# Ordinary products for the left half's last pairs, a skewed right half, and activation sums and two weight sums on GpSimd, in a two-layer hybrid decoder

## The chip, the cores and the metric

The kernel runs on one core of a Trainium2 chip. The metric is the device time of one execution in microseconds. PE is TensorE, DVE VectorE, ACT ScalarE, POOL GpSimd and SP SyncE, whose queue issues nearly all DMA transfers.

## The reference

Two layers over 256 tokens of width 2048, in float32. Every layer computes

```
h  = RMSNorm(x)
P  = h @ W_in            # [q | k | v | gate_B | gate_C | conv_in]
A  = differential attention(q, k, v)
Cv = gate_B * causal_conv3(gate_C * conv_in)
x  = x + concat([A, Cv]) @ W_out
x  = x + (relu(RMSNorm(x) @ W_up) ** 2) @ W_down     # W_up 2048x8192, W_down 8192x2048
```

The change touches only the last line, the MLP.

## The kernel before

**Precision.** Each float32 operand of a matmul is split into a high part (a rounding copy on ACT, the "h" or "hi" tiles) and a low part (a subtraction on DVE, the "l" or "lo" tiles). A product is three matmuls, `TERMS` = high x high, high x low, low x high. So every weight that comes from HBM costs one ACT copy and one DVE subtraction of the same size (L281 and L282 for the projections and w_down's right half, L692 and L693 for w_up, L707 and L708 for the left half's forms).

**The walk over pairs.** `mlp` goes over 8192 hidden columns in NP = 32 pairs of 128. For a pair i, `up_column` computes two columns a and b of 128 (32 matmuls each, in two halves of 8 k-tiles, weights from `Weights.take`), into a PSUM bank "av" of which there is one; `evict` copies it by ACT and adds its two parts by DVE (L788). `square` then makes relu, the factor of the norm (L796) and the square, writes the result to DRAM by POOL's queue (`hid`, L799), makes four sums S1 to S4 of 128x128 on DVE (L800 to L803) and splits all eight matrices into f (L805 on ACT, L806 on DVE).

**The left half's products.** Columns 0 to 1023 of the output are made by a scheme with seven products for a 2x2 block product instead of eight. The weights' side of pair j needs a 512-column block split for b11, b21, b22 (`plain`), sums t of the weight blocks (`sums`: L724 makes t[:, 0:2], L727 and L728 the other two), and their splits t13 and t24 (L707, L708). The 21 matmuls of pair j = i - LAG, with LAG = 2, stand behind the columns of pair i: four products behind column a, three behind column b. The seven results stay in seven PSUM banks over the whole walk. Two pairs of products remain after the last columns. Then `onto` and additions combine them into x.

**The right half.** Columns 1024 to 2047 are ordinary products: for each pair, `back` reads hid from DRAM, ACT and DVE split it (L885, L886), and 24 matmuls (L892) go into two accumulators of two banks. Weights come as `draw` tiles of 256 rows by 1024 columns (1 MB).

**What sets the order.** PE's order is that of the program text. The orders of DVE, ACT, POOL and SP are set by a scheduler when the program is built, except for instructions marked `late`, which stay in program order. Each engine then goes through its own queue strictly in order. `Weights` keeps a list of jobs (`column`, `plain`, `sums`, `more`, `rows`) and makes AHEAD = 3 of them ahead of their use. `wpool` has three buffers each for hi and lo. A tile of a pool that was opened where another pool had closed can be written only when the old pool's users are done: `upool` (w_up's raw tiles), `spool` (split forms and t), `fpool` (h and f) and `dpool` (draw) are opened in this order at the start of the MLP, over the projections' pools.

Of the kernel before, what the change touches and what calls it, by code (L numbers as in the profile page):

```python
# [9 lines left out]
F32 = mybir.dt.float32  # L10
# [24 lines left out]
LAG = 2  # L35

# [64 lines left out]
def trunk(ctx: ExitStack, tc: tile.TileContext, x, w_in, w_out, conv_w, q_norm_g, k_norm_g,  # L101
# [564 lines left out]
    def mlp(l, mnorm, last):  # L666
# [3 lines left out]
        with ExitStack() as scope:  # L670
            upool = scope.enter_context(tc.tile_pool(name="upool", bufs=3))
            spool = scope.enter_context(tc.tile_pool(name="spool", bufs=1))
# [5 lines left out]
            weights = Weights(upool)  # L678
            raws, forms = {}, {}
# [24 lines left out]
            def parts(src, tag, bufs):  # L704
                hi = spool.tile(list(src.shape), F32R, tag=f"{tag}h", name=f"{tag}h", bufs=bufs)
                lo = spool.tile(list(src.shape), F32R, tag=f"{tag}l", name=f"{tag}l", bufs=bufs)
                nc.scalar.activation(hi, src, AF.Copy)  # L707
                nc.vector.tensor_sub(lo, src, hi.bitcast(F32))  # L708
                return hi, lo

            def quarters(i):


                def plain():
                    raw = forms["raw"] = load_rows(i, 0).rearrange("p k (n c) -> p k n c", n=2)
                    h1, l1 = parts(raw[:, 0, 0], "b1", 2)
                    h2, l2 = parts(raw[:, 1], "b2", 1)
                    return (h1, l1), (h2[:, 0], l2[:, 0]), (h2[:, 1], l2[:, 1])

                def sums():  # L720
                    raw = forms["raw"]
                    t = forms["t"] = spool.tile([P, 4, CH], F32, tag="t", name="t")

                    nc.vector.tensor_sub(t[:, 0:2], raw[:, :, 1], raw[:, 0])  # L724
                    h, lw = parts(t[:, 0:2], "t13", 1)

                    nc.vector.tensor_add(t[:, 2], t[:, 1], raw[:, 0, 0])  # L727
                    nc.vector.tensor_sub(t[:, 3], raw[:, 1, 0], t[:, 2])  # L728
                    return (h[:, 0], lw[:, 0]), (h[:, 1], lw[:, 1])

                def more():
                    h, lw = parts(forms["t"][:, 2:4], "t24", 1)
                    return (h[:, 0], lw[:, 0]), (h[:, 1], lw[:, 1])

                return plain, sums, more

            def rows(i, k, box):
                def make():
                    if k == 0:
                        box.append(load_rows(i, 2 * CH))  # L740
# [3 lines left out]
            for i in range(NP + LAG):  # L744
                plain, sums, more = quarters(i - LAG)
                if i < NP:
                    column(i, 0, 0)
                    column(i, 0, 1)
                if i >= LAG:
                    weights.jobs += [plain, sums]  # L750
                if i < NP:
                    column(i, 1, 0)
                    column(i, 1, 1)
                if i >= LAG:
                    weights.jobs.append(more)
            for i in range(NP):
                box = []
# [4 lines left out]
            hid = [dram.tile([P, 2 * S], F32, name=f"hid{l}{i}") for i in range(NP)]  # L762

            def up_column(name, warm):


                acc = (bank(name) if warm else ps.tile([P, CH], F32, tag="av", name=name, bufs=1))
                acc = acc.rearrange("p (h s) -> p h s", h=2)
                for kh in range(2):
                    hi, lo = weights.take()  # L770
                    for part, wt in ((0, hi), (1, lo)):
                        for k in range(8):
                            a = mT[kh * 2 + k // KG]
                            while not a.ready:
                                work.tick()
                            nc.tensor.matmul(  # L776
                                acc[:, 0] if part else acc, wt[:, k],
                                a.ap[:, 0, k % KG] if part else a.ap[:, :, k % KG],
                                start=(part == 0 and kh == 0 and k == 0),
                                stop=(part == 1 and kh == 1 and k == 7), skip_group_check=True)  # L780
                            if k % 4 == 3:
                                work.tick()
                return acc

            def evict(acc, dst):
                ev = nat.tile([P, 2, S], F32, tag="wide", name="ev")
                nc.scalar.activation(ev, acc, AF.Copy)
                nc.vector.tensor_add(dst, ev[:, 0], ev[:, 1])  # L788

            def square(i, h):  # L790
# [8 lines left out]
                nc.gpsimd.dma_start(hid[i], u)  # L799
                nc.vector.tensor_add(h[:, S1], h[:, A21], h[:, A22])  # L800
# [4 lines left out]
                nc.scalar.activation(f[:, 0], h, AF.Copy)  # L805
                nc.vector.tensor_sub(f[:, 1], h, f[:, 0].bitcast(F32))  # L806
                return f

            prods = []

            def product(n, i, a, b):

                f = fs[i]
                for m, (pa, pw) in enumerate(TERMS):
                    nc.tensor.matmul(prods[n], f[:, pa, a], b[pw], start=(i == 0 and m == 0),  # L815
                                     stop=(i == NP - 1 and m == 2))

            fs = {}
            h = None
            for i in range(NP + LAG):  # L820
                j = i - LAG
                if i < NP:
                    h = fpool.tile([P, 8, P], F32, tag="h", name="h", bufs=1)
                    evict(up_column(f"up{l}{i}a", i < LAG),
                          h[:, 0:2].rearrange("p a c -> p (a c)"))
                if j == 0:
                    wides = [mm.tile([P, 2, CH], F32, tag="mm2", name=f"pr{l}{n}")
                             for n in range(2)]
                    prods += [wides[0][:, 0], wides[0][:, 1], wides[1][:, 0], wides[1][:, 1]]
                    prods += [bank(f"pr{l}{n}") for n in (5, 6, 7)]  # L830
                if j >= 0:
                    b11, b21, b22 = weights.take()
                    t1, t3 = weights.take()
                    product(0, j, A11, b11)
                    product(1, j, A12, b21)
                    product(2, j, S4, b22)
                    product(4, j, S1, t1)
                    work.tick()
                if i < NP:
                    evict(up_column(f"up{l}{i}b", i < LAG),  # L840
                          h[:, 2:4].rearrange("p a c -> p (a c)"))
                    fs[i] = square(i, h)
                if j >= 0:
                    t2, t4 = weights.take()
                    product(6, j, S3, t3)
                    product(5, j, S2, t2)
                    product(3, j, A22, t4)
                    work.tick()


            p1, p2, p3, p4, p5, p6, p7 = prods
# [5 lines left out]
            e1 = wide("e1")  # L857
            nc.scalar.activation(e1, p1, AF.Copy, scale=mnorm.scale)
            onto(xs[0][:, 0], p2, xs[0][:, 0])
            onto(xs[1][:, 0], p3, xs[1][:, 0])  # L860
            onto(xs[0][:, 1], p4, xs[0][:, 1])
            u2, u3, u4 = wide("u2"), wide("u3"), wide("u4")
            onto(u2, p6, e1)
            onto(u3, p7, u2)
            onto(u4, p5, u2)
            onto(xs[1][:, 1], p5, xs[1][:, 1])
            for dst, v in ((xs[0][:, 0], e1), (xs[1][:, 0], u4), (xs[0][:, 1], u3),
                           (xs[1][:, 1], u3)):
                nc.vector.tensor_add(dst, dst, v)
            if last:  # L870
                for n in range(2):
                    for t in range(NT):
                        nc.sync.dma_start(
                            out[0, t * P:(t + 1) * P, n * CH:(n + 1) * CH], xs[n][:, t])
# [5 lines left out]
            acc = [mm.tile([P, NT, CH], F32, tag="mm2", name=f"dn{l}{n}") for n in range(2)]  # L880
            for i in range(NP):
                back = nat.tile([P, 2, S], F32, tag="wide", name="back")
                nc.sync.dma_start(back.rearrange("p k s -> p (k s)"), hid[i])
                f = fpool.tile([P, 2, 2, S], F32R, tag="f", name="fr")
                nc.scalar.activation(f[:, 0], back, AF.Copy)  # L885
                nc.vector.tensor_sub(f[:, 1], back, f[:, 0].bitcast(F32))  # L886
                for k in range(2):
# [63 lines left out]
```

## Time and profile before

| what | us |
|---|---|
| median of 3 runs | 2214.55 (2214.05 to 2215.54) |
| the profiled execution | 2216.24 |
| its span | 2214.4 |
| mean granted TensorE clock | 0.989 of full speed |

The span is the time from the first to the last instruction; 1.84 us lie around it. The page gives each engine's busy time; PE's instructions are pipelined, so that a matmul shows 0.39 us but follows its predecessor by 0.227 to 0.229 us. The marks of layer 0 in the trace: the o projection ends at 398.97, the last up column of the walk at 905.41, the first matmul of the right half starts at 932.52. In layer 1 the last up column ends at 2008.04, the first matmul of the right half starts at 2031.12, and the last accumulation ends at 2211.24. The lines "idle before <-releaser" in the timeline tell how long an engine stood still before an instruction and which engine's instruction ended that.

### The profile page before, as it was taken

Reading aid. Unit: us, or ns where it says so; the run is one execution under the profiler, and the core shown is the slowest. Engines: PE = TensorE matmul, PEld = TensorE weight load, DVE = VectorE, ACT = ScalarE, POOL = GpSimd, SP = SyncE. Lnnn points to the kernel's source line nnn. Section 1 sums busy time; section 2 is a strip of 40 time slices with the busy share of each in tenths; the row PEclk is TensorE's granted clock in tenths of the full one; section 3 lists DMA queues with packets and bytes.
Section 4 is the critical chain, followed back from the end, with each engine's and each line's share of the span. In section 5 each row is a group of like instructions: output and inputs, shape, how many; then the busy total and the mean of one; then the engine's idle time right before and its main releaser. Section 6 shows DMA issues by size and latency. Waiting matters only on the chain.

```text
span 2214.4 us, 29244 instructions
## 1 busy us (share of the span) xinstructions
PE 2167.4 (98%) x11054; PEld 1836.7 (83%) x11054; DVE 1631.7 (74%) x2303; ACT 1296.1 (59%) x1758; POOL 130.7 (6%) x186
## 2 busy tenths in 40 slices
PE   8999999999999999799999999999999999998999
PEld 6888888788888888688878888887888888886887
DVE  6677655789898989665556776557989898987555
ACT  6455445566666666454454654446666666664443
POOL 2021200000000000000010111000000000000000
PEclk9999999999999999899999999999999999998999
DMA  7656666566766666477565566656666666665774
GB/s 259 180 153 194 202 185 180 190 218 206 221 211 217 215 212 202 166 234 241 185 191 180 159 197 197 188 164 205 217 212 216 215 213 219 211 198 161 244 244 164
DMA packets 280717, 446.64 MB, mean 202 GB/s; under 512 B 10915, under 2 KB 191733, under 8 KB 280576
## 3 DMA queue, kind: packets, MB, share of 16 engines
q1 hardware_dynamic: 273872, 423.66, 61.7%
q0 software_dynamic: 6656, 21.10, 2.5%
q8 instruction: 86, 1.41, 0.3%
q14 instruction: 55, 0.45, 0.1%
q10 hardware_dynamic: 48, 0.02, 0.0%
HBM read 425.84 MB, written 18.90 MB: 201 GB/s over the span
## 4 chain that ended last, share of the span: by engine, by line
PE 96%; DMA 1%; DVE 1%; ACT 0%; issue 0%; POOL 0%; SPq 0%; DVEq 0%
PE dn L892 16%; PE pr L815 14%; PE o L337 8%; PE gc L359 4%; PE ci L359 4%; PE q L337 4%; PE gb L359 4%; PE v L337 4%; PE k L337 4%; DMA draw<-in_w_down_dram 1%; PE sc L499 1%; PE av L535 1%; PE tpn L401 0%; DVE wlo L282 0%; PE ptp L525 0%; PE up00b L776 0%
## 5 line engine op out<-in xcount | busy, mean ns | idle before, releaser
L282 DVE TENSOR_TENSOR wlo<-raw,whi 128x1024 fp32r<-128x1024 f32 (+1 forms) x258 | 317.1, 1231 | 244.3 <-ACT whi L281 243.1
L281 ACT ACTIVATE whi<-raw 128x1024 fp32r<-128x1024 f32 (+1 forms) x258 | 271.3, 1053 | 311.8 <-PE o L337 73.6
L692 ACT ACTIVATE uhi<-uraw 128x1024 fp32r<-128x1024 f32 x256 | 270.6, 1057 | 304.4 <-PE o L337 10.0
L693 DVE TENSOR_TENSOR ulo<-uraw,uhi 128x1024 fp32r<-128x1024 f32 x256 | 312.6, 1221 | 110.9 <-ACT uhi L692 106.7
L892 PE MATMUL dn<-whi,fr 128*128 128x512 f32 x1024 | 319.9, 393 | 9.5 <-ACT fr L885 7.0
L282 DVE TENSOR_TENSOR wlo<-draw,whi 128x1024 fp32r<-128x1024 f32 x128 | 156.9, 1225 | 150.7 <-ACT whi L281 150.6
L281 ACT ACTIVATE whi<-draw 128x1024 fp32r<-128x1024 f32 x128 | 135.7, 1061 | 174.4 <-PE dn L892 168.4
L892 PEld LDWEIGHTS dn<-whi,fr 128*128 128x128 f32 x1024 | 194.3, 190 | 51.4 <-ACT fr L885 7.9
L892 PE MATMUL dn<-wlo,fr 128*128 128x512 f32 x512 | 200.8, 392 | 0.0
L337 PE MATMUL o<-whi,cat 128*128 128x512 f32 x512 | 159.6, 390 | 0.0
L892 PEld LDWEIGHTS dn<-wlo,fr 128*128 128x128 f32 x512 | 97.2, 190 | 20.1
L337 PEld LDWEIGHTS o<-whi,cat 128*128 128x128 f32 x512 | 96.1, 188 | 19.8
L815 PE MATMUL pr<-t13h,f 128*128 128x512 f32 x256 | 100.5, 395 | 0.0
L337 PE MATMUL o<-wlo,cat 128*128 128x512 f32 x256 | 99.6, 389 | 0.0
L799 POOL DMA_DIRECT2D hid<-h x64 | 34.8, 544 | 985.4 <-ACT h L798 985.4
L815 PE MATMUL pr<-b2h,f 128*128 128x512 f32 x256 | 91.4, 398 | 0.0
L337 PE MATMUL q<-whi,nT 128*128 128x512 f32 x256 | 87.0, 409 | 3.3 <-ACT nT L247 2.1
L815 PE MATMUL pr<-t24h,f 128*128 128x512 f32 x256 | 89.6, 391 | 0.0
L337 PE MATMUL k<-whi,nT 128*128 128x512 f32 x256 | 85.3, 399 | 0.0
L337 PE MATMUL v<-whi,nT 128*128 128x512 f32 x256 | 83.4, 396 | 0.0
L708 DVE TENSOR_TENSOR t24l<-t,t24h 128x1024 fp32r<-128x1024 f32 x64 | 78.4, 1225 | 3.5 <-ACT t24h L707 0.4
L708 DVE TENSOR_TENSOR t13l<-t,t13h 128x1024 fp32r<-128x1024 f32 x64 | 78.4, 1224 | 3.5 <-ACT t13h L707 1.5
(953 smaller groups left out, 4667.8 us busy)
## 6 DMA issues: line engine op xcount, KB each, us to landing
uraw<-in_w_up_dram SPq DMA_DIRECT2D x128, 1024.0 KB, 5.8
draw<-in_w_down_dram SPq DMA_DIRECT2D x128, 1024.0 KB, 5.1
raw<-in_w_in_dram SPq DMA_DIRECT2D x192, 512.0 KB, 3.9
raw<-in_w_out_dram SPq DMA_DIRECT2D x64, 512.0 KB, 3.6
hid<-h POOLq DMA_DIRECT2D x64, 256.0 KB, 3.5
back<-hid SPq DMA_DIRECT2D x64, 256.0 KB, 2.7
rev<-by_dist_d POOLq DMA_DIRECT2D x4, 1024.0 KB, 10.6
out_dram<-x SPq DMA_DIRECT2D x8, 256.0 KB, 2.3
```

Of the source, the lines that this page charges most:

```text
L281: nc.scalar.activation(hi[:, k], raw[:, k], AF.Copy)
L282: nc.vector.tensor_sub(lo[:, k], raw[:, k], hi[:, k].bitcast(F32))
L337: nc.tensor.matmul(acc[:, t], a.ap[:, pa, k % KG, t * P:(t + 1) * P], (hi, lo)[pw][:, j], start=(k == 0 and n == 0), stop=(k == nk - 1 and ...
L359: nc.tensor.matmul(acc[:, f, 0] if part else acc[:, f], wt[:, k % 4, fs], a.ap[:, 0, k % KG] if part else a.ap[:, :, k % KG], start=(part ...
L499: nc.tensor.matmul(sc[:, :W], qT[m * DK:(m + 1) * DK, a, i, t * P:(t + 1) * P], kT[m * DK:(m + 1) * DK, b, i, :W], start=(n == 0), stop=(n ...
L535: nc.tensor.matmul(av[:, i * P:(i + 1) * P], pT[:, a, k * P:(k + 1) * P], v[:, b, k, i * P:(i + 1) * P], start=(k == 0 and n == 0), stop=( ...
L692: nc.scalar.activation(hi, src, AF.Copy)
L693: nc.vector.tensor_sub(lo, src, hi.bitcast(F32))
L708: nc.vector.tensor_sub(lo, src, hi.bitcast(F32))
L799: nc.gpsimd.dma_start(hid[i], u)
L815: nc.tensor.matmul(prods[n], f[:, pa, a], b[pw], start=(i == 0 and m == 0), stop=(i == NP - 1 and m == 2))
L892: nc.tensor.matmul(acc[n][:, t], f[:, pa, k, t * P:(t + 1) * P], b[pw][:, n], start=(i == 0 and k == 0 and m == 0), stop=(i == NP - 1 and ...
```

## The change

The change has six parts, all of them in `mlp`.

1. The last LAG = 2 pairs of the left half are ordinary products (eight products, 24 matmuls, instead of seven and 21), after the last up column; pairs 0 to 29 keep the seven products.
2. The right half goes in 16 blocks of 512 rows. Its two 512-column halves n = 0 and n = 1 are skewed: (0,0), (1,0), (0,1), (2,0), (1,1) and so on. Weights come as 512 KB chunks (`weights.straight`), hid as 512 KB blocks. The half n = 0 ends one block before n = 1.
3. POOL makes S1 to S4 (four 128x128 operations for a pair) and t[:, 0:2] (now two operations of 128x512), and the four additions of the products to x.
4. The columns of pair 0 are computed with the k-half as the outer loop, in one tile with two accumulators, and the splits and sums of pair 0 are `late`.
5. The draw load of pair i + 1 is issued in `sums` of pair i.
6. `fpool` and `dpool` are opened first, then a stack `first` with `spool` and `upool`, which is closed ahead of the right half; `rpool` and `gpool` (the right half's chunks and blocks) then take its place.

```diff
+            fpool = scope.enter_context(tc.tile_pool(name="fpool", bufs=2))
+            dpool = scope.enter_context(tc.tile_pool(name="dpool", bufs=2))
+            first = scope.enter_context(ExitStack())
+            spool = first.enter_context(tc.tile_pool(name="spool", bufs=1))
+            upool = first.enter_context(tc.tile_pool(name="upool", bufs=3))
...
-                    nc.vector.tensor_sub(t[:, 0:2], raw[:, :, 1], raw[:, 0])
+                    for m in range(2):
+                        keep(nc.gpsimd.tensor_tensor(t[:, m], raw[:, m, 1], raw[:, 0, m],
+                                                     op=ALU.subtract))
                     h, lw = parts(t[:, 0:2], "t13", 1)
...
+                    if i + 1 < NP - LAG:
+                        loads[i + 1]()
...
             for i in range(NP):
+                pair = quarters(i - LAG)
+                if i == 0:
+                    for kh in range(2):
+                        for c in range(2):
+                            column(0, c, kh)
+                    continue
...
+            order = [(b - n, n) for b in range(NB2 + 1) for n in range(2) if 0 <= b - n < NB2]
+            for b, n in order:
+                weights.straight(w_down[l], b * KG * P, KG, (2 + n) * CH)
...
-                nc.vector.tensor_add(h[:, S1], h[:, A21], h[:, A22])
-                nc.vector.tensor_sub(h[:, S2], h[:, S1], h[:, A11])
-                nc.vector.tensor_sub(h[:, S3], h[:, A11], h[:, A21])
-                nc.vector.tensor_sub(h[:, S4], h[:, A12], h[:, S2])
+                n = 4
+                if i < NP - LAG:
+                    n = 8
+                    for dst, a, b, op in ((S1, A21, A22, ALU.add), (S2, S1, A11, ALU.subtract),
+                                          (S3, A11, A21, ALU.subtract),
+                                          (S4, A12, S2, ALU.subtract)):
+                        nc.gpsimd.tensor_tensor(h[:, dst], h[:, a], h[:, b], op=op)
...
+            first.close()
+            rpool = scope.enter_context(tc.tile_pool(name="rpool", bufs=RAW))
+            gpool = scope.enter_context(tc.tile_pool(name="gpool", bufs=3))
+            weights.pool = rpool
...
+            for dst, v in ((x11, e1), (x12, e4), (x21, e3), (x22, e3)):
+                nc.gpsimd.tensor_tensor(dst, dst, v, op=ALU.add)
...
+            for j in range(NP - LAG, NP):
+                for k in range(2):
+                    b = weights.take()
+                    for n, t, p in ((0, 0, 2), (0, 1, 4), (1, 0, 3), (1, 1, 8)):
+                        for m, (pa, pw) in enumerate(TERMS):
+                            nc.tensor.matmul(
+                                prods[p], fs[j][:, pa, 2 * k + t], b[pw][:, n],
+                                start=(p == 8 and j == NP - LAG and k == 0 and m == 0),
+                                stop=(j == NP - 1 and k == 1 and m == 2))
```

In the queues of the changed program the two parts that moved to POOL stand as follows. At the start of the walk: hid(0), the sums of pair 0, hid(1), the sums of pair 1, t of pairs 0, 1 and 2, hid(2), the sums of pair 2. In the walk, for each pair: hid, two sums, two operations of t for a later pair, two sums. On ACT, the square of pair 1 stands behind the eviction of the first column of pair 2, and the split t13 of pair 0 behind that square and f(1). The first three loads of w_up in a layer wait for the end of the o projection, and the first two draw loads stand ahead of them on SP.

More of the change, by code (lines that the diff above doesn't have):

```diff
@@ L733, in more @@
                     return (h[:, 0], lw[:, 0]), (h[:, 1], lw[:, 1])
+                loads[i] = load
                 return plain, sums, more
@@ L759, in mlp, with column_bank, up_part @@
                 rows(i, 1, box)
[L762 to L783, printed above, removed]
+            order = [(b - n, n) for b in range(NB2 + 1) for n in range(2) if 0 <= b - n < NB2]
+            for b, n in order:
+                weights.straight(w_down[l], b * KG * P, KG, (2 + n) * CH)
+            hid = [dram.tile([P, KG * S], F32, name=f"hid{l}{b}") for b in range(NB2)]
+            def column_bank():
+                acc = ps.tile([P, CH], F32, tag="av", name="upc", bufs=1)
+                return acc.rearrange("p (h s) -> p h s", h=2)
+            def up_part(acc, kh):
+                hi, lo = weights.take()
+                for part, wt in ((0, hi), (1, lo)):
+                    for k in range(8):
+                        a = mT[kh * 2 + k // KG]
+                        while not a.ready:
+                            work.tick()
+                        nc.tensor.matmul(
+                            acc[:, 0] if part else acc, wt[:, k],
+                            a.ap[:, 0, k % KG] if part else a.ap[:, :, k % KG],
+                            start=(part == 0 and kh == 0 and k == 0),
+                            stop=(part == 1 and kh == 1 and k == 7), skip_group_check=True)
+                        if k % 4 == 3:
+                            work.tick()
             def evict(acc, dst):
@@ L814, in product @@
+            prods = {}
+            def product(n, j, a, b, stop=False):
                 for m, (pa, pw) in enumerate(TERMS):
-                    nc.tensor.matmul(prods[n], f[:, pa, a], b[pw], start=(i == 0 and m == 0),
-                                     stop=(i == NP - 1 and m == 2))
+                    nc.tensor.matmul(prods[n], fs[j][:, pa, a], b[pw], start=(j == 0 and m == 0),
+                                     stop=(stop and m == 2))
             fs = {}
-            h = None
-            for i in range(NP + LAG):
+            for i in range(NP):
@@ L821, in mlp @@
                 j = i - LAG
[L822 to L851, printed above, removed]
+                end = i == NP - 1
+                h = fpool.tile([P, 8, P], F32, tag="h", name="h", bufs=1)
+                if i == 0:
+                    two = mm.tile([P, 2, CH], F32, tag="mm2", name="up0")
+                    two = [two[:, c].rearrange("p (h s) -> p h s", h=2) for c in range(2)]
+                    for kh in range(2):
+                        for c in range(2):
+                            up_part(two[c], kh)
+                            if kh:
+                                evict(two[c], h[:, 2 * c:2 * c + 2])
+                    fs[0] = square(0, h)
+                    continue
@@ new lines, in mlp @@
+                for c in range(2):
+                    if i < LAG:
+                        acc = bank("upw").rearrange("p (h s) -> p h s", h=2)
+                    else:
+                        acc = column_bank()
+                    up_part(acc, 0)
+                    up_part(acc, 1)
+                    evict(acc, h[:, 2 * c:2 * c + 2])
+                    if c == 1:
+                        fs[i] = square(i, h)
+                    if j == 0 and c == 0:
+                        for pair in ((1, 6), (2, 3)):
+                            w2 = mm.tile([P, 2, CH], F32, tag="mm2", name=f"pr{l}{pair[0]}")
+                            prods[pair[0]], prods[pair[1]] = w2[:, 0], w2[:, 1]
+                        for n in (4, 5, 7):
+                            prods[n] = bank(f"pr{l}{n}")
+                    if j >= 0 and c == 0:
+                        b11, b21, b22 = weights.take()
+                        t1, t3 = weights.take()
+                        product(1, j, A11, b11, end)
+                        product(2, j, A12, b21)
+                        product(3, j, S4, b22)
+                        product(5, j, S1, t1, end)
+                        work.tick()
+                    elif j >= 0:
+                        t2, t4 = weights.take()
+                        product(7, j, S3, t3, end)
+                        product(6, j, S2, t2, end)
+                        product(4, j, A22, t4)
+                        work.tick()
@@ L853, in onto @@
+            blocks = {0: block(0)}
             def onto(dst, p, base):
@@ L870, in mlp, with store @@
+            for dst, p in ((x11, 2), (x21, 4), (x12, 3), (x22, 8)):
+                onto(dst, prods[p], dst)
+            def store(n):
+                for t in range(NT):
+                    nc.sync.dma_start(
+                        out[0, t * P:(t + 1) * P, n * CH:(n + 1) * CH], xs[n][:, t])
             if last:
[L871 to L874, printed above, removed]
+                store(0)
+                store(1)
@@ L877, in mlp @@
                 work.start(norm.chunk(1, 2), 24)
[L880 to L887, printed above, removed]
-                    b = weights.take()
-                    for n in range(2):
+            accs = {}
+            for b, n in order:
+                if n == 0:
+                    if b + 1 < NB2:
+                        blocks[b + 1] = block(b + 1)
+                if b == 0:
+                    accs[n] = mm.tile([P, NT, CH], F32, tag="mm2", name=f"dn{l}{n}")
+                f, acc = blocks[b], accs[n]
+                for kp in range(KG // 2):
+                    hi, lo = weights.take()
+                    for k in (2 * kp, 2 * kp + 1):
                         for t in range(NT):
```

113 lines of the change are left out of this document (56 added, 57 removed).

## Prediction

> **What bounds the kernel now.** I read the page's shares and chain first, then the waits of PE, then the timeline of one steady pair and of each seam.
>
> ```profile
> PE 2167.4 (98%) x11054; PEld 1836.7 (83%) x11054; DVE 1631.7 (74%) x2303; ACT 1296.1 (59%) x1758; POOL 130.7 (6%) x186
> ...
> PE 96%; DMA 1%; DVE 1%; ACT 0%; issue 0%; POOL 0%; SPq 0%; DVEq 0%
> ```
>
> PE is the path. Only two things shorten it: fewer matmuls, or fewer gaps. The waits of PE show the gaps:
>
> ```profile
> PE pr L815 <- ACT f L805: 9.8, 2, 5.0
> PE dn L892 <- ACT fr L885: 7.0, 2, 5.6
> PE up00a L776 <- DVE nT L248: 4.7, 2, 3.7
> PE up10a L776 <- DVE nT L248: 4.6, 2, 3.6
> ...
> PE tpn L401 <- DVE nT L248: 3.0, 1, 3.0
> PE dn L892 <- DVE fr L886: 2.5, 1, 2.5
> ```
>
> (total, times, longest). They lie at three seams, none in the walk over the pairs. PE's timeline at layer 0's seam before the right half:
>
> ```profile
> 904.81 0.76 PE L776 MATMUL up031b<-nT,ulo 128*128 128x256 f32 x5
> ...
> 918.64 0.79 PE L815 MATMUL pr<-b1h,f 128*128 128x512 f32 x1 [4.80 <-ACT f L805]
> ...
> 932.52 0.80 PE L892 MATMUL dn<-whi,fr 128*128 128x512 f32 x1 [5.55 <-ACT fr L885]
> ```
>
> After each long idle some 14 matmuls come 0.427 us apart instead of 0.227: 2.8 us more, so a gap costs more than its wait.
>
> Last, DVE in a steady pair (two of its operations, and its only idle):
>
> ```profile
> 703.03 0.28 DVE L800 TENSOR_TENSOR h<-h 128x128 f32<-128x128 f32 x1
> ...
> 703.44 1.22 DVE L724 TENSOR_TENSOR t<-draw 128x1024 f32<-128x1024 f32 x1
> ...
> 714.61 1.23 DVE L693 TENSOR_TENSOR ulo<-uraw,uhi 128x1024 fp32r<-128x1024 f32 x1 [1.62 <-ACT uhi L692]
> ```
>
> A pair takes 15.93 us on PE (two up columns of 5.56, 21 products of 0.229). DVE is idle for 1.62 of it, so busy 14.31.
>
> **The seam before the right half: -29 us.** The last column ends at 905.41. 51 products x 0.227 = 11.6 should end at 917.0. The right half, counted back from 939.10 by its 16 matmuls at 0.228, begins in effect at 935.45: 18.4 lost. Layer 1: 2008.04 + 11.6 = 2019.65 against 2035.54, 15.9 lost. After: pair 29's nine products, then 48 ordinary ones, so the right half starts 57 x 0.227 = 12.9 us after the column. That is 6 products more than before, 1.36 us. Pair 31's f is needed at 33 x 0.227 = 7.5; its chain (eviction 0.6, addition 0.42, relu 0.54, ratio 0.42, square 0.54, f 0.54, 0.6) sums to 3.7, some 6 with hand-overs and other work in the queues. Blocks and straight chunks can load only after the products' pool is free, at 2.05: 512 KB takes 3.9 (the raw row), the two splits 1.05 + 1.22, so 8.2 to 9 against 12.9. Both fit. Saved: (18.4 + 15.9) - 2 x 1.36 = 31.6; up to 6 off for slips, I take 29 (25 to 31). The cover is those 48 products; where it fails, the rival below.
>
> **Layer boundary and end: -5.7.** Between the layers 6.25 is lost (idles of 1.1 and 3.0 and the slow start after them). With the first 512 columns finished a block (24 matmuls, 5.5 us) earlier, most of the norm's chain and one PSUM buffer come earlier: -5 (-3 to -6). At the end two of four accumulations of about 0.7 go behind PE's last block: -0.7.
>
> **The start of the MLP: +5.** The stacks of pools change places: the buffers of the up weights now lie where the projections' tiles were, so SP issues the first three up loads only when the o phase is done. In the profile that moment is 399.21, where the draw load L699 with the same wait was issued. In exchange draws come early, at about 393. A 1 MB up load lands 5.8 after issue: 405.0 to 406, uhi 1.06, so PE starts at about 406.5 instead of 398.97. That idle is 7.5; with 2.8 of slow matmuls, less 1.1 of transposes that it covers, 9.2 is lost. Before, the stretch 398.97 to 412.49 held 6.64 of work, so 7.0 (layer 1: 6.6) was lost. Net +2.4 per layer (0 to +5). The order with k-half outermost hides the last nT, which caused the old idle.
>
> **The first product of t13: +19.** This is a new wait. POOL's queue has hid(1), the four sums of pair 1, and only then t(0); ACT's has square(1) behind the eviction of pair 2's first column. From the end of that column: the eviction ends at 0.75, square at 1.3, POOL starts at 1.6, issues hid for 0.54 (L799 row), four sums at 0.3 to 0.4 each (bounds 0.20 from the 128x4 rows of POOL, 0.61 from its 128x256 row), two halves of t at 1.29 (POOL's 128x512 row, L645), then t13h 1.05. That is 7.4 if nobody interferes. DVE's split of f(1) falls between the halves of t: about 1.1 more, 8.5. PE has nine products, 2.06, as cover: 6.4 idle, about 1 for t13l, 2.8 of slow matmuls, less what overlaps: 9.5 per layer (8 to 11). Before, t came from DVE early and there was no wait. Queued behind t13h on ACT are t24h and the next uhi; five later microseconds of column cover those.
>
> **The steady pairs: +4.** DVE loses four sums (0.81 by their starts) and L724 (1.13): 12.37 stays. POOL gets 4 x 0.3 to 0.4 and 2 x 1.29: 3.8 to 4.2 of work. Alone both fit in 15.93. Together they may not:
>
> ```profile
> 211.26 1.29 POOL L645 TENSOR_TENSOR gc01w<-gc01w,rowb 128x512 f32<-128x512 f32 x1 [1.47 <-PE ci L359]
> ```
>
> ```profile
> 211.31 2.33 DVE L282 TENSOR_TENSOR wlo<-raw,whi 128x1024 fp32r<-128x1024 f32 x1 [0.19 <-ACT whi L281]
> ```
>
> DVE's split took 2.33 instead of 1.23 because it began 0.05 after POOL's product: it stood still for 1.1 of POOL's 1.29. Elsewhere POOL's L582 took 4.42 against three splits back to back. So the two run in turn, each hand-over saving about 0.14. All DVE operations of a pair are of that kind (two SBUF tensors). Then a pair costs DVE 12.37 + 2 x 1.15 + 4 x 0.2 = 15.5, against 15.93. It fits by 0.4 us, and PE has three weight tiles of reserve. I take the row's hand-over (nearest, the same pair of engines) and 0.07 us in each of 60 pairs for places where the order catches them badly: +4 in all (0 to +37).
>
> The Trainium skill says the same of the pair: in "SBUF — State Buffer", section "Who interferes with whom", a DVE instruction with two SBUF inputs contends with a GpSimd one that reads SBUF, and the first to start holds it for the whole instruction. The trace agrees in kind (2.33 against 1.23); by the page's whole-instruction lock no hand-over is saved, which is the first rival. "GPSIMD Engine Reference", section "Engine selection", also advises VectorE for elementwise work, GpSimd being about twice as slow; here 1.29 against 0.68 for 128x512.
>
> **The sum.** -29 - 5.7 + 5 + 19 + 4 = -6.7 on the profiled span of 2214.4: 2207.7. That execution took 2216.24, 1.84 around its span and 1.7 above the median of 2214.55; I take the change from the median: 2207.9, say 2208. The likeliest case's own range, with its terms not all at the same end, is 2200 to 2218.
>
> **Rival 1: DVE and POOL become the bound (slower).** If the hand-over saves nothing, a pair costs 12.37 + 2.58 + 1.6 (sums at 0.40) = 16.55, 0.62 above 15.93; from 15.93 on every pair is late. 60 pairs give +37, in place of +4: 2241. For it: only 0.4 us of room, and POOL's results feed DVE's own next steps. Against: the 0.14 seen at each hand-over. Chance 0.22.
>
> **Rival 2: the new waits at the start are small (faster).** If t(0) reached ACT before the column ended, or up loads were on chip when the o phase ends, the 24 go: 2184 for both, 2194 for half. The queue order speaks against it: hid(1) stands ahead of t(0). Chance 0.13.
>
> **Rival 3: the seam stays (slower).** If the first block or straight chunk is split later than 12.9 us after the column, PE idles there as it did. Each microsecond counts once, with 2.8 more from some 4 us on. With the old idle of 5.6 + 2.8 in both layers, +17 on the forecast: 2225. For it: these loads cannot be issued before 2.05, and ACT and DVE are then busy with pair 31 and the products' evictions. Against: 4 us of slack. Chance 0.15.
>
> **How the numbers follow.** A measurement of this kernel tells about 0.2% (4.4 us) from no change. The forecast has 0.50: 2200 to 2218 reaches over both bounds, and I give 0.30 of it to faster, 0.14 to the same, 0.06 to slower. With rival 2's 0.13 faster has 0.43; with 0.02 of the weak form of rival 3 the same has 0.16; the rest, 0.22 + 0.13 + 0.06, is 0.41 slower. Cases of both signs hold most of the chance. The range reaches from half of rival 2, 2194, to a little past rival 1, 2246.
>
> **What would show it.** Right: PE's waits of pr on f and of dn on fr fall under 2 us per layer; the first up column waits 7 to 8 us for uhi; one wait of 5 to 7 us per layer for t13h; steady pairs of 15.9 to 16.0 us; DVE operations in them now and then 0.3 to 1.2 longer. Wrong: a pair period of 16.5 (rival 1), no wait for t13h (rival 2), dn still waiting for its blocks (rival 3), or a wait at pairs 3 and 4 that I have not costed.

## Result and the profile after

The changed kernel is slower: 2233.88 us (2233.57 to 2234.50, 4 runs) beside 2215.05 for the kernel before on the same chip, ratio 1.0082 (95% interval 1.0070 to 1.0095). The forecast was 2208, inside a range of 2194 to 2246: the sign was wrong, the range held the time. Of the rivals, the first (DVE and GpSimd become the bound) came true in its mechanism; its time was 2241.

The page's busy times and PE's waits (total, times, longest) of the changed kernel:

```profile
PE 2175.4 (97%) x11066; PEld 1831.5 (82%) x11066; DVE 1700.5 (76%) x1929; ACT 1260.7 (56%) x1718; POOL 451.4 (20%) x554
```

```profile
PE up L799 <- ACT uhi L694: 18.0, 2, 9.2
PE pr L839 <- ACT t13h L714: 14.7, 2, 7.4
PE upc L799 <- ACT ev L809: 7.8, 39, 0.2
```

DVE executes 374 instructions fewer and is busy 69 us longer; an operation that stands still counts as busy. The waits on f and fr at the seam before the right half are gone. Three others are there: the first up column for its weights, the first t13, and, new, some 40 short waits for the eviction of a pair's first column.

Stage by stage, from the starts of PE's matmuls in both traces (from one mark to the next, layer 0 and layer 1; the right half's start before the change is counted back over its slow matmuls, as in the prediction):

| stage | before | after | difference | forecast |
|---|---|---|---|---|
| end of o phase to the third column's end (first products) | 36.07, 35.66 | 40.82, 42.00 | +11.1 | +5 |
| from there to the end of the last column: first t13 | | | +20.9 | +19 |
| the same: the later pairs | | | +20.5 | +4 |
| last column to right half | 30.04, 27.50 | 13.95, 13.97 | -29.6 | -29 |
| right half of layer 0 to end of next o phase | 566.56 | 560.57 | -6.0 | -5 |
| right half of layer 1 to the end of the span | 178.86 | 178.97 | +0.1 | -0.7 |

With +0.5 from before the MLP this makes +17.5; the spans of the two profiled executions differ by 17.4 (2214.4 and 2231.8), the medians by 18.8. The stretch of the pairs is 470.37 before and 491.04 after in both layers. It splits by the distance from one pair's first product to the next: the first is 26.72 and 25.99 instead of 15.93, the next seven to nine are 15.93, and from about the tenth on all are 16.43.

One such pair on DVE and GpSimd, and the PE wait in it:

```profile
709.14 1.23 DVE L715 TENSOR_TENSOR t24l<-t,t24h 128x1024 fp32r<-128x1024 f32 x1 [0.18 <-ACT t24h L714]
710.61 6.17 DVE L695 TENSOR_TENSOR ulo<-uraw,uhi 128x1024 fp32r<-128x1024 f32 x2 [0.25 <-ACT uhi L694]
716.70 0.68 DVE L715 TENSOR_TENSOR b1l<-draw,b1h 128x512 fp32r<-128x512 f32 x1
```

```profile
710.50 0.89 POOL L828 TENSOR_TENSOR h<-h 128x128 f32<-128x128 f32 x2
711.34 2.53 POOL L734 TENSOR_TENSOR t<-draw 128x512 f32<-128x512 f32 x2
713.84 1.86 POOL L828 TENSOR_TENSOR h<-h 128x128 f32<-128x128 f32 x2
```

```profile
712.05 2.12 PE L799 MATMUL upc<-nT,uhi 128*128 128x512 f32 x8 [0.20 <-ACT ev L809]
```

Two splits that take 2.35 us back to back take 6.17: DVE stands still for 3.8 us, while GpSimd does five of its six operations, and the two lie one behind the other. Nearly all of it falls on the first split alone:

```profile
710.61 4.77 DVE L695 TENSOR_TENSOR ulo<-uraw,uhi 128x1024 fp32r<-128x1024 f32 x1 [0.25 <-ACT uhi L694]
```

It starts 0.11 after GpSimd's first sum and gets on only when the fifth operation ends, at 714.29. DVE's other operations in the pair follow each other with next to no gap; its only idle is 0.18 + 0.25. DVE is full, its later work comes late, so ACT's copies do, and PE's next column waits for the eviction that clears its only bank. DVE repeats every 16.4 from the third pair on, PE at first every 15.93: the split t24l starts 13.3 us before PE uses its result, half a microsecond less with each pair, and 9.55 from about the tenth on. This lead is the reserve that covers the first pairs.

### The profile page after: what moved, and what is told of

Same layout as the page of the kernel before. It is cut to its first block, busy times and chain, and to the rows that moved or that the text cites. A ratio compares the mean times of both kernels' runs of the same rounds, so it can differ in the third digit from the quotient of the medians.

```text
span 2231.8 us, 29487 instructions
## 1 busy us (share of the span) xinstructions
PE 2175.4 (97%) x11066; PEld 1831.5 (82%) x11066; DVE 1700.5 (76%) x1929; ACT 1260.7 (56%) x1718; POOL 451.4 (20%) x554
## 5 line engine op out<-in xcount | busy, mean ns | idle before, releaser
L283 DVE TENSOR_TENSOR wlo<-raw,whi 128x1024 fp32r<-128x1024 f32 (+1 forms) x386 | 473.3, 1227 | 385.8 <-ACT whi L282 384.5
L695 DVE TENSOR_TENSOR ulo<-uraw,uhi 128x1024 fp32r<-128x1024 f32 x256 | 517.5, 2038 | 45.0 <-ACT uhi L694 44.2
L799 PE MATMUL upc<-nT,uhi 128*128 128x512 f32 x1920 | 485.9, 395 | 8.0 <-ACT ev L809 7.8
L799 PEld LDWEIGHTS upc<-nT,uhi 128*128 128x128 f32 x1920 | 351.4, 189 | 92.6 <-ACT ev L809 25.6
L960 PE MATMUL dn<-whi,g 128*128 128x512 f32 x1024 | 316.4, 389 | 0.0
L799 PEld LDWEIGHTS upc<-nT,ulo 128*128 128x128 f32 x1920 | 262.1, 190 | 19.1
L799 PE MATMUL upc<-nT,ulo 128*128 128x256 f32 x1920 | 267.7, 282 | 0.0
L960 PEld LDWEIGHTS dn<-whi,g 128*128 128x128 f32 x1024 | 192.2, 188 | 39.9
L960 PE MATMUL dn<-wlo,g 128*128 128x512 f32 x512 | 199.2, 389 | 0.0
L828 POOL TENSOR_TENSOR h<-h 128x128 f32<-128x128 f32 x240 | 162.2, 690 | 6.0
```

The source lines that it names most:

```text
L283: nc.vector.tensor_sub(lo[:, k], raw[:, k], hi[:, k].bitcast(F32))
L799: nc.tensor.matmul(acc[:, 0] if part else acc, wt[:, k], a.ap[:, 0, k % KG] if part else a.ap[:, :, k % KG], start=(part == 0 and kh == 0 ...
L828: nc.gpsimd.tensor_tensor(h[:, dst], h[:, a], h[:, b], op=op)
L960: nc.tensor.matmul(acc[:, t], f[:, pa, k, t * P:(t + 1) * P], (hi, lo)[pw][:, k % 2], start=(b == 0 and k == 0 and m == 0), stop=(b == NB2 ...
```

## Experiments

Theory A: DVE and GpSimd work in turn (one stands still while the other works), and their total in a pair exceeds 15.93. Theory B: GpSimd is only slow, and what hangs on its results comes late. Ratios are against the kernel before on the same chip.

**Sums and t on DVE.**

```diff
-                        nc.gpsimd.tensor_tensor(h[:, dst], h[:, a], h[:, b], op=op)
+                        nc.vector.tensor_tensor(h[:, dst], h[:, a], h[:, b], op=op)
...
-                    for m in range(2):
-                        keep(nc.gpsimd.tensor_tensor(t[:, m], raw[:, m, 1], raw[:, 0, m],
-                                                     op=ALU.subtract))
+                    keep(nc.vector.tensor_sub(
+                        t[:, 0:2], raw[:, :, 1],
+                        raw[:, 0]))
```

> The changed kernel with the four sums (L828) and t[:, 0:2] (L734) back on DVE; all else as changed. Theory A (DVE and GpSimd take turns, which made the pairs 16.43 us): every pair of the walk is 15.93 again, which gives back 9.7 us in each layer. Theory B (GpSimd is only slow, its results come late): the same period, so this run does not part A from B, it only sizes the two. The wait for the first t13h: if GpSimd's queue makes it, as the prediction said, it goes (10.8 us in layer 0, 10.1 in layer 1), and the kernel takes 2233.9 - 19.4 - 20.9 = 2193.6. If the order does (t of pair 0 is kept in program order and stands behind f of pair 1 on DVE), some 5.5 us of idle and 2.8 of slow matmuls stay per layer, and it takes about 2210.

2211.56, ratio 0.9979 (0.9970 to 0.9989). All pairs after the first are 15.93. But the wait for the first t13h stayed, if a little shorter (the first distance fell from 26.7 and 26.0 to 24.8 and 25.4); the same waits of PE as above:

```profile
PE pr L839 <- ACT t13h L714: 11.5, 2, 5.8
PE pr L839 <- DVE t13l L715: 2.2, 2, 1.4
```

So GpSimd's queue is not needed for that wait. Here DVE's queue makes it, whose timeline shows f of pair 1 directly ahead of t of pair 0:

```profile
445.17 1.22 DVE L831 TENSOR_TENSOR f<-h,f 128x1024 fp32r<-128x1024 f32 x1
446.30 1.22 DVE L733 TENSOR_TENSOR t<-draw 128x1024 f32<-128x1024 f32 x1
```

**Only t on DVE.** The edit is the second half of the one above.

> The changed kernel with t[:, 0:2] back on DVE, the sums on GpSimd. Theory A: DVE 12.37 + 1.13 and GpSimd's four sums at 0.45, less a little at the hand-overs, 15.2 of 15.93: pairs of 15.93 all through the walk, -19.4. Theory B, with the sums on the path from square to f: pairs stay above 15.93. The wait for t13h as in the run with all on DVE.

2297.45, ratio 1.0363 (1.0345 to 1.0380): the slowest of all, with nearly all pairs at 17.5. Theory A's sum (15.2) failed here. ACT's timeline, and PE's wait:

```profile
715.77 1.06 ACT L830 ACTIVATE f<-h 128x1024 fp32r<-128x1024 f32 x1 [2.28 <-POOL h L828]
716.73 0.58 ACT L809 ACTIVATE ev<-upc 128x512 f32<-128x512 f32 x1
```

```profile
717.37 2.11 PE L799 MATMUL upc<-nT,uhi 128*128 128x512 f32 x8 [1.27 <-ACT ev L809]
```

Here the scheduler put f ahead of the eviction on ACT. f waits for GpSimd's sums, four of which took 5.09 us between DVE's splits, and PE's next column waits for the eviction behind f.

**Pair 0 not kept in order.**

```diff
-                keep = late if i == 0 else lambda ins: None
+                keep = lambda ins: None
```

> The changed kernel with the splits and sums of pair 0 not kept in program order (part 4 of the change undone in that one point); sums and t still on GpSimd. If that order makes the wait for the first t13h: t of pair 0 now stands ahead of hid(0) in GpSimd's queue and the wait goes, -20.9 at most. The pairs at 16.43 stay, and since the reserve built up during the wait is gone they may start earlier than the tenth pair: up to 10 more pairs per layer at +0.5, +10 in all. So 2213 to 2223. If GpSimd's queue and not this order makes the wait: no change, 2234.

2214.08, ratio 0.9989 (0.9980 to 0.9999). The wait for t13h is gone; the distance of the first two pairs is 15.94. The pairs at 16.43 stay and begin at the tenth again, so the reserve that covers the first nine does not come from that wait. In GpSimd's queue t of pair 0 now runs at 400.3, long ahead of hid(0).

**Three mended at once.** The first and the third edit (sums and t on DVE, pair 0 not kept in order), and:

```diff
+            upool = scope.enter_context(tc.tile_pool(name="upool", bufs=3))
             fpool = scope.enter_context(tc.tile_pool(name="fpool", bufs=2))
             dpool = scope.enter_context(tc.tile_pool(name="dpool", bufs=2))
             first = scope.enter_context(ExitStack())
             spool = first.enter_context(tc.tile_pool(name="spool", bufs=1))
-            upool = first.enter_context(tc.tile_pool(name="upool", bufs=3))
```

> Three things at once: sums and t on DVE, pair 0 not kept in program order, and the pool of the raw up weights opened first in the MLP, as it was before the change. Kept from the change: ordinary last pairs, skewed right half, pair 0 with the k-half outermost. By the stage table: the walk as before (-19.4), no wait for t13h (-20.9), the start of the MLP at most as late as before (-11.1, or more where the k-half order hides the last nT: the old loss there was 7.0 and 6.6). 2233.9 - 51.4 = 2182.5 down to 2170. If what the seam before the right half gained hangs on GpSimd having taken work from DVE, it comes out at 2190 or more.

2188.91, ratio 0.9877 (0.9862 to 0.9892); above the 2170 to 2182.5 that the stage table gave. PE waited again for the last nT (10.9 in two waits), as before the change. DVE's timeline shows why: t of pair 0 waits for its draw load, and an nT stands behind it.

```profile
413.01 1.23 DVE L733 TENSOR_TENSOR t<-draw 128x1024 f32<-128x1024 f32 x1 [4.58 <-DMA draw<-in_w_down_dram]
414.15 0.48 DVE L249 SCALAR_TENSOR_TENSOR nT<-tpn,gains,nT 128x256 fp32r<-128x256 f32 x1
```

So the `late` of pair 0 does what it is there for, and its price was that t went too far back.

**Only the sums on DVE.** The first half of the first edit.

> The changed kernel with the four sums back on DVE, t[:, 0:2] on GpSimd. Theory A (turns on one shared resource, the sum of both engines' work decides): DVE 12.37 + 0.81, GpSimd 2 x 1.27, 15.7 of 15.93, so pairs of 15.93 or little above. Theory B (GpSimd's results come late on a path that PE waits for, as in the run with t alone on DVE, where f stood ahead of the eviction on ACT and waited for GpSimd's sums): f no longer waits for GpSimd, and the t13 split has a pair's time, so 15.93 too; B is told from A by the next two runs. Time 2233.9 - 19.4 - about 2 per layer of shorter wait for the first t13h = 2211.

2242.74, ratio 1.0122 (1.0106 to 1.0137); missed by 32. Pairs are 16.44 almost from the start, though DVE is idle for 1.10 in one of them, waiting for uhi. As with t alone on DVE, f stands ahead of the eviction on ACT, waiting 1.22 for DVE's sums (three of them 1.86, stopped by GpSimd). That this order makes the 16.44 here is read from the trace, not tried; in its sibling it is tried below.

**GpSimd work that nobody waits for.** To the version with all on DVE are added, behind each pair's hid (with a scratch tile z, cleared once):

```diff
+                for m in range(2):
+                    late(nc.gpsimd.tensor_tensor(z[:, 2], z[:, 0], z[:, 1], op=ALU.subtract))
...
```

> The kernel with sums and t on DVE (2211.6), to which GpSimd adds, behind each pair's hid, two subtractions of 128x512 between scratch tiles that nobody reads. No instruction waits for them. Theory A: DVE's 14.31 and GpSimd's 2.5 make 16.8 in a pair against 15.93: up to +0.9 in each of some 20 to 30 pairs of a layer, 2245 to 2265, and single DVE splits of 2.3 us and more. Theory B (only results that come late cost time): 2211.6, pairs of 15.93.

2258.85, ratio 1.0195 (1.0175 to 1.0215), against 0.9979 without it. From about the sixth pair on the distance is 16.6. GpSimd's timeline, and DVE's beside it:

```profile
749.06 2.83 POOL L825 TENSOR_TENSOR z<-z 128x512 f32<-128x512 f32 x2
```

```profile
748.84 1.89 DVE L831 TENSOR_TENSOR h<-h 128x128 f32<-128x128 f32 x2
750.65 2.31 DVE L734 TENSOR_TENSOR t<-draw 128x1024 f32<-128x1024 f32 x1
```

Two sums, elsewhere 0.49, took 1.89, and t 2.31 instead of 1.22: DVE lost 2.5 us to results that nobody uses. Theory B alone can't do that.

**The same with memsets.** `nc.gpsimd.memset(z[:, 2], 0.0)` in place of the subtraction.

> The same with two memsets of 128x512 on GpSimd in place of the subtractions: they write and read nothing. If only GpSimd operations that read SBUF stop DVE (the Trainium skill, SBUF - State Buffer, Who interferes with whom, states so): 2211.6, pairs of 15.93 and DVE splits of 1.23. If any GpSimd operation on SBUF does: longer DVE splits, and pairs above 15.93 if the memsets are longer than 0.8 us each.

2212.36, ratio 0.9984 (0.9973 to 0.9994), as without them; all later pairs 15.93. The same view:

```profile
751.71 1.13 POOL L825 MEMSET z<- 128x512 f32 x2
```

```profile
751.42 0.49 DVE L831 TENSOR_TENSOR h<-h 128x128 f32<-128x128 f32 x2
751.82 1.22 DVE L734 TENSOR_TENSOR t<-draw 128x1024 f32<-128x1024 f32 x1
```

DVE isn't slowed at all. Two memsets are shorter than two subtractions (1.13 and 2.83), but they overlap DVE's sums and t, which keep their 0.49 and 1.22. In a steady pair the queues of ACT and DVE hold the same order in this run, in the one with subtractions and in the one with neither, so no order explains the difference between them.

**The start mended.** The joined version, with `late` for pair 0 again, its splits and sums made behind the square of pair 0 (both are wrapped so that they are made once; that part of the edit is left out here):

```diff
                     fs[0] = square(0, h)
+                    for make in forms["pair0"]:
+                        make()
                     continue
...
```

> The joined version, but with pair 0 kept in program order again and its splits and sums made already behind the square of pair 0, instead of behind that of pair 1. In the joined version the last nT stood behind t of pair 0 and its draw load on DVE (PE idle 5.9 and 5.0, with slow matmuls after). By the queues t of pair 0 now stands behind all nT and ahead of f of pair 1, so both waits go: 2188.9 - 10.9 - some 2 to 4 of slow matmuls = 2174 to 2176. If the late draw load then holds up t13 of pair 0 at the third column: 2185 or more.

2177.33 (2176.97 to 2178.03), ratio 0.9827 (0.9810 to 0.9843). It is the fastest version: 38 us below the kernel before, 56 below the changed one. Both waits of the start are gone. Some 2 to 3 us remain in each layer in the first five pairs (16.31, 16.37 and 17.22 in layer 0), partly waits for f. By stages, against the kernel before: the seam -29.5, the start of the MLP -9.7, the layer boundary -5.1, the pairs +5.0 and +1.1 before the MLP, together -38.2.

**Skew undone** in that version:

```diff
-            order = [(b - n, n) for b in range(NB2 + 1) for n in range(2) if 0 <= b - n < NB2]
+            order = [(b, n) for b in range(NB2) for n in range(2)]
```

> The mended version (2177.3) with the right half's blocks in plain order, (0,0), (0,1), (1,0) and so on: only the skew is undone, blocks and chunks stay. If the skew makes the gain at the layer boundary and the end (5.9 and 0.6 in the changed kernel): 2183 to 2184, with the idles ahead of q and the transposes back. If the smaller chunks and earlier buffers do: 2177 to 2178.

2178.35, ratio 0.9829 (0.9814 to 0.9843): no difference beyond the noise. The skew as such is worth nothing here.

**Both halves ending together**, unskewed, the loops over k and n interleaved:

```diff
+                for kp in range(KG // 2):
+                    both = [weights.take(), weights.take()]
+                    for k in (2 * kp, 2 * kp + 1):
+                        for n in range(2):
...
```

> The mended version, unskewed, with the two halves of the right half taken in turn for every 128 rows, so that they end 6 matmuls apart (before the change 6 too, in the unskewed run 24, in the changed kernel 48). Chunks of 512 KB, blocks and pools stay. If a half that ends early makes the gain at the layer boundary: PE idles there again, up to 6 in all, 2182 to 2184. If something else does (smaller chunks, the place of the pools): 2177 to 2179.

2184.14, ratio 0.9856 (0.9840 to 0.9873), some 6 us more than unskewed. Of these the layer boundary has 4.4: its stage takes 565.6 instead of 561.1 (566.6 before the change), with PE's idle at the transposes back:

```profile
PE tpn L402 <- DVE nT L249: 3.3, 1, 3.3
```

One half has to end early; 24 matmuls are enough, 48 give no more.

**Seven products for all pairs** in the mended version (the loop over the last pairs takes the seven products ahead of `first.close()`, their sums and forms are made as for the others, and the right half's chunks are held back until the pool is closed):

> The mended version with seven products in all 32 pairs, so that the last two pairs' 42 matmuls stand behind the last column as before the change: only the ordinary products are undone (and with them the early end of the split forms' pool). If the 48 ordinary matmuls are what covers f of the last pairs and the first loads of the right half: the seam costs 27 to 33 us again instead of 14, in both layers, less 1.4 for six matmuls saved: 2177.3 + 26 to 38 = 2203 to 2215. If the smaller first block and chunks alone shorten the seam: below 2190.

2209.29, ratio 0.9969 (0.9956 to 0.9982): 32 us more. PE's waits:

```profile
PE dn L976 <- DVE g L928: 16.8, 2, 8.4
PE pr L849 <- ACT f L840: 5.2, 2, 2.6
```

Six matmuls more per layer (1.36 us) buy about 17. They do it in two ways that this run undoes together: the ordinary products cover f of the last pairs, and they need no split forms, so that the pool closes ahead of them. The first block of the right half is loaded 2.3 us after the last column in the mended version and 17.5 and 18.3 after it here. How the 17 is shared between the two was not tried.

**The eviction ahead of f** in the version with t on DVE, the sums on GpSimd:

```diff
+                    ev = copy(acc)
+                    if c == 0:
+                        fs[i - 1] = finish(todo)
...
```

`copy` is the eviction's ACT part, `finish` the split of f taken out of `square`; both are kept in this order.

> The version with t on DVE and the sums on GpSimd (2297, pairs of 17.5), with one thing moved: on ACT the eviction of a pair's first column stands ahead of f of the pair before, not behind it. GpSimd's sums take as long as they did. If the period of 17.5 comes from that order (f waits for the sums, the eviction for f, the next column for the eviction): pairs of 15.93 to 16.1, and 2215 to 2222. If it comes from DVE and GpSimd being short of time together: pairs stay above 17.

2199.33, ratio 0.9920 (0.9903 to 0.9936): 98 us less, and better than forecast. All but a few pairs are 15.93, although GpSimd's sums take 1203 ns each on average. The first distances fell as well, from 27.22 and 26.11 to 17.72 and 20.07: t of pair 0 and its t13h now run ahead of f of pair 1. So the 17.5 was the order on ACT, not a want of time.

**The same order in the changed kernel** (sums and t on GpSimd):

> The changed kernel (sums and t on GpSimd) with the order on ACT that mended the pairs of 17.5: the eviction of a pair's first column, then f of the pair before. If the total of both engines makes its 16.43 (DVE 12.37 and some 3.9 in which GpSimd stops it, with waits 16.4): pairs of 16.3 to 16.5 remain, 2225 to 2236. If an order on ACT makes it: pairs of 15.93, 2200 to 2214.

2233.60, ratio 1.0075 (1.0059 to 1.0090): unchanged, pairs of 16.43. This run tries nothing new in the steady pairs, for the scheduler had already put f behind that eviction in the changed kernel. ACT's timeline there:

```profile
711.43 0.57 ACT L809 ACTIVATE ev<-upc 128x512 f32<-128x512 f32 x1
715.73 1.06 ACT L830 ACTIVATE f<-h 128x1024 fp32r<-128x1024 f32 x1 [2.26 <-POOL h L828]
```

DVE's timeline of this run is that of the changed kernel too:

```profile
793.80 1.23 DVE L715 TENSOR_TENSOR t24l<-t,t24h 128x1024 fp32r<-128x1024 f32 x1 [0.18 <-ACT t24h L714]
795.27 6.17 DVE L695 TENSOR_TENSOR ulo<-uraw,uhi 128x1024 fp32r<-128x1024 f32 x2 [0.25 <-ACT uhi L694]
```

So f ahead of the eviction, which made the 17.5, is not what makes the 16.43. With both parts on GpSimd the total decides; with t alone on DVE, the order on ACT did; for the sums alone on DVE that order is only read.

## Why the prediction was wrong

**Steady pairs: the step that failed most.** It said that DVE and GpSimd fit into 15.5 of 15.93 and took +4; measured +20.5, which is 16.5 of the 24 us by which the sum was off. The mechanism was named, its size was not. The step took two 1.15 and four 0.2 for GpSimd, 3.1 in all, from a hand-over that would save 0.14 each time. DVE in fact stood still for 3.8: five operations went by before the first split got on (4.77 instead of 1.23), with no hand-over between them. One of the step's own rows could have warned of it. For "the two run in turn" it cites L582 against three splits:

```profile
229.18 3.49 DVE L282 TENSOR_TENSOR wlo<-raw,whi 128x1024 fp32r<-128x1024 f32 x3
229.41 4.42 POOL L582 TENSOR_TENSOR cv<-cv,rowb 128x512 f32<-128x512 f32 x1 [16.86 <-ACT whi L281]
```

The three splits take their usual time, and GpSimd's operation waits through all of them and ends 1.2 after the last. That is not turn by turn. A sum of 128x128 takes GpSimd 0.45 undisturbed, above the estimate of 0.3 to 0.4. The step also left out the 0.43 in which DVE waits for ACT. With these the pair of 16.43 divides into 3.8 of standing still, 0.43 of idle and 12.2 of DVE's own work, beside the 12.37 of the sum. Rival 1 had 16.55 for the pair, but charged 60 of them; some twenty of 29 distances in a layer paid, because the first nine drew on the lead. This step alone did not turn the sign: with its +4 the change would have come out at +1, no change, and most of the rest came from the start of the MLP.

**The page's rule.** By "SBUF — State Buffer", section "Who interferes with whom", of the Trainium skill, the loser blocks for the whole instruction. The runs agree in kind: DVE lost 1.09 on its operation for t beside an unused GpSimd subtraction of 1.44. In the changed kernel it lost 3.8, as much as GpSimd's five operations took from 710.50 to 714.29. They also bear out that a GpSimd operation that only writes stops nothing.

**The first t13: size and chain right (+20.9 against +19), the root missed.** In the changed kernel GpSimd's queue makes this wait, as the prediction said:

```profile
442.56 2.68 POOL L828 TENSOR_TENSOR h<-h 128x128 f32<-128x128 f32 x4
445.20 3.50 POOL L734 TENSOR_TENSOR t<-draw 128x512 f32<-128x512 f32 x2
448.74 1.06 ACT L714 ACTIVATE t13h<-t 128x1024 fp32r<-128x1024 f32 x1 [2.41 <-POOL t L734]
```

The split t13h starts as soon as GpSimd has t, 8.5 us after the column's end, where the prediction had its end; the four sums took 2.68 instead of 1.2 to 1.6. What the prediction missed is why t stands there. Pair 0 is kept in program order, and that puts its t behind the work of pair 1 on whichever engine makes it: behind the sums on GpSimd, behind f on DVE, where 5.8 of the wait stayed. Without `late` the wait went with t still on GpSimd, and with `late` but the forms made earlier it went with t on DVE.

**The start of the MLP: +11.1 against +5.** The wait was foreseen, too short (8.8 and 9.2 idle against 7.5). The first up load landed 7.5 and 7.9 after its issue instead of the 5.8 of the median row, with a draw load and two more up loads under way. The -1.1 for transposes was wrong: they did not move into the idle but stand behind the first matmuls. The old loss of 7.0 is 6.9 by the prediction's own marks.

**The seam, the boundary and the end.** At the seam -29.6 against -29: the sum of 31.6 less an allowance for slips, which was a guess and happened to fit: 2 us did slip (13.95 instead of 12.9 in each layer, 0.7 of it a wait of PE for a split). The run with seven products shows that the ordinary products pay, through the cover that was named and the earlier close of the pool together. At the boundary -6.0 against -5; that one half ends early is the cause, as written, but the skew isn't needed for it. At the end nothing came of the -0.7: from PE's last matmul to the end of DVE's last accumulation it is 1.45 us in both kernels, so only two accumulations stood behind PE before the change as well.

## What to carry over

Before work is moved to an engine because it is idle, add up what it takes from the engine that it is to relieve: for two-input elementwise operations on SBUF, GpSimd's time here came off DVE's almost whole (3.8 of some 4.4), and 0.5 us too much in a pair of 16 cost 20 of the 36 us that the seam and the boundary had gained. Then look at what is queued behind whoever waits for the slow engine: one copy in the wrong place on ACT was worth 98 us. And test the parts of a change apart: what is left of this one without GpSimd's sums and t is worth 38 us, once the pools' order and the place of pair 0's forms are mended.

## What the runs showed of the hardware

A GpSimd subtraction of two SBUF tiles of 128x512 (1.3 us) stops a DVE operation of the same kind for 1.1 to 1.4 us, whether anyone needs its result or not; a GpSimd memset of 0.54 us stops it not at all. Which engine gets in between the other's operations varies, and no run here shows by what rule. With t alone on DVE, GpSimd got in about once for each DVE operation: four sums of 0.45 took 5.09 us between DVE's splits. But one split waited through five GpSimd operations (4.77), and one GpSimd operation through three splits (4.42). The granted clock was 1.000 in the mended version, with and without the skew and with both halves ending together, where PE stands still for at most 1.6 us at a time in the walk and at the seams before the right half, and 0.992 in the changed kernel, where each long idle was followed by matmuls 0.43 us apart.
